# Where the first low weight part of the next stage stands at the end of the second and third feed-forward net

## The chip, the cores and the metric

The kernel runs on one core of one Trainium2 chip. The metric is device time in microseconds (us), the median over runs of the same program. Engines are named as in the profile: PE is TensorE (matmuls) and PEld its weight loads, DVE is VectorE, ACT is ScalarE, POOL is GpSimd, SP is SyncE, which here only issues DMA transfers. L76 is line 76 of the kernel before.

## The reference

Two layers act on 256 tokens of 1024 features, in float32. Each layer is a feed-forward net, a mixer, a cross-attention and a second feed-forward net, each added to its input and normalised:

```python
for l in range(DEPTH):                       # DEPTH = 2
    h = layer_norm(ALPHA * h + 0.5 * swiglu(h, ffn1_gate[l], ffn1_up[l], ffn1_down[l]), ...)
    z = h @ w_in[l]                          # conv, recurrence and pooling branches on slices of z
    ...
    h = layer_norm(ALPHA * h + mix, ...)
    h = layer_norm(ALPHA * h + cross_attn(h, mem, ca_q[l], ca_k[l], ca_v[l], ca_o[l]), ...)
    h = layer_norm(ALPHA * h + 0.5 * swiglu(h, ffn2_gate[l], ffn2_up[l], ffn2_down[l]), ...)

def swiglu(x, w_gate, w_up, w_down):         # 1024 -> 2816 -> 1024
    return (jax.nn.silu(x @ w_gate) * (x @ w_up)) @ w_down
```

The four nets in order of time are called net 1 and 2 (`ffn1`, `ffn2` of layer 0) and net 3 and 4 (of layer 1). The keys of the cross-attention come from `mem` and not from `h`, so their products need nothing of the net in front of them.

## The kernel before

**High and low parts.** Every float32 operand of a matmul is used as two parts. `split` (L74) makes them: ScalarE rounds the tile to the high part (`whi`, L75) and VectorE subtracts that from the source for the low part (`wlo`, L76). A product of two such operands is three matmuls (`mm_rows`, L156): high by high, high by low, low by high. The tensor named `acc` holds most sums, `dn` those of the nets' last products.

**Weights.** `load` (L79) brings a block of weights in two or four tiles of 128 x 1024 through a ring of six raw buffers, one transfer of 512 KB each on SP's queue, and splits each tile into one of eight `whi` and one of eight `wlo` buffers. A raw buffer is free for the next transfer when its low part is made; a `whi` or `wlo` buffer is free when TensorE has done its last matmul with it.

**The end of a net.** A net's products run over 512 hidden features at a time. Its last three slabs of down weights, six tiles of high and low parts, are kept in `end` (L849 to L859). `finish` (L326) then works through the two tiles of 128 tokens: `tile_done(0)`, then `tile_done(1)`. For each tile TensorE adds the last products (`tail`, L861), and VectorE adds the old `h` to each half of the features as the sums are done (L356), forms the mean (`mv`, L366), waits for ScalarE's sum of squares (L369), forms `rs` (L370, and a power on POOL, L374), scales (L377) and shifts (L382, the list `normed`). During tile 1's last products TensorE transposes the finished tile 0 (L199, called from L354), and the split of that gives the next stage's `xT`. `finish` returns a function that transposes tile 1 later, within the next stage (`pend`).

**The next stage.** Behind net 2 comes `first` of net 3 (L503): `load` of four gate tiles and four up tiles, then for token tile 0 the eight gate products and the first four up products, the transposes of tile 1 (`pend`, L584), and the rest. Behind net 3 comes `keys(1, 0)` (L883): `load` of four key tiles, then products with `mem`, the transposes of tile 1 among them, and then the mixer's first projection, whose weights `columns` (L911) queues behind tile 1's norm.

**What sets the order.** Each engine works through its own queue in order. The order in a queue is made ahead of time by a planner, which takes the instructions that are ready by its own estimate of times, the earlier traced one first. `tc.issue_after(ins)` adds to that: what a block traces on `ins`'s engine is queued behind `ins`. The kernel before has one such rule for the place of this change. Where the net has three blocks done by seven products instead of eight (`5 in sevens`: nets 2, 3 and 4) and it isn't the last, `finish` gets `ordered=True`: the work of tile 1 on VectorE, and the four low parts of the next block that is loaded, are queued behind tile 0's norm. The list `guard` carries that instruction from `finish` to the next `load`:

```python
first = guard.pop() if guard else None                       # L84, load
...
with tc.issue_after(first) if first else nullcontext():      # L116
    split(h, w, r)
...
tile_done(0)                                                 # L389, finish
with tc.issue_after(normed[-1].ins) if ordered else nullcontext():
    if ordered:
        guard.append(normed[-1].ins)
    tile_done(1)
```

The rule holds the low parts alone: the rounding is on ScalarE, on which `issue_after` of a VectorE instruction lays nothing.

Of the kernel before, what the change touches and what calls it, by code (L numbers as in the profile page):

```python
# [18 lines left out]
DEPTH = 2  # L19
# [4 lines left out]
NK = DM // P  # L24
# [4 lines left out]
CHUNK = 512  # L29
# [31 lines left out]
def model(ctx: ExitStack, tc: tile.TileContext, t: dict, out: bass.AP):  # L61
# [7 lines left out]
        return ps.tile(list(shape), F32, tag=tag, name=tag)  # L69


    loads, normed, lows, turns, guard = [], [], [], [], []

    def split(hi, lo, src):  # L74
        rounded = nc.scalar.copy(hi, src)  # L75
        lows.append(nc.vector.tensor_tensor(lo, src, hi.bitcast(F32), op=ALU.subtract))  # L76
        return rounded

    def load(src, k0, nk, c0, ncol, fine=False, dealt=False, across=False):  # L79


        hi, lo, todo = [], [], []
        step = 2048 // ncol
        first = guard.pop() if guard else None  # L84
        for a in range(k0, k0 + nk, step):
            half = step // 2
            raw = [
                wp.tile([P, 1024], F32, tag="raw", name="raw", bufs=6).rearrange("p (k c) -> p k c", c=ncol)
                for _ in range(2)
            ]  # L90
            part = 1 if fine else half
            for b in range(0, step, part):
                to = raw[b // half][:, b % half : b % half + part, :]
                if dealt:

                    c, u = divmod(a // 2, 2)
                    at = slice(c * CHUNK + 2 * P * b, c * CHUNK + 2 * P * (b + 1))
                    rows = src[at, c0 : c0 + ncol].rearrange("(p u) c -> p u c", u=2)[:, u, :]
                    loads.append(nc.sync.dma_start(to[:, 0, :], rows))
                elif across:  # L100
                    rows = src[:, c0 : c0 + ncol].rearrange("(p k) c -> p k c", p=P)
                    loads.append(nc.sync.dma_start(to, rows[:, a + b : a + b + part, :]))
                else:
                    loads.append(nc.sync.dma_start(
                        to, src[(a + b) * P : (a + b + part) * P, c0 : c0 + ncol].rearrange("(k p) c -> p k c", p=P)
                    ))
            for s in range(2):
                h = wp.tile([P, 1024], F32R, tag="whi", name="whi", bufs=8)
                w = wp.tile([P, 1024], F32R, tag="wlo", name="wlo", bufs=8)
                h = h.rearrange("p (k c) -> p k c", c=ncol)  # L110
                w = w.rearrange("p (k c) -> p k c", c=ncol)
                r = raw[s]
                if fine:
                    todo += [(h[:, b, :], w[:, b, :], r[:, b, :]) for b in range(half)]
                else:
                    with tc.issue_after(first) if first else nullcontext():  # L116
                        split(h, w, r)
                hi.append(h)
                lo.append(w)
        return Weights(hi, lo, half, todo)  # L120
# [50 lines left out]
    h = [cst.tile([P, DM], F32, name=f"h{i}") for i in range(NT)]  # L171
# [32 lines left out]
    def transposed(src, i, dh, dl, unit=idn, keep=None):  # L204
        for j in range(2):
            transposed_half(src, i, j, dh, dl, unit, keep)
# [116 lines left out]

    squares = kTh[:, 4:8, :].rearrange("p k c -> p (k c)")

    def finish(mm, y, scale, gb, units, last=False, junk=None, ordered=False):  # L326

        g, b = gb
        def tile_done(i):

            st = sm.tile([P, 4, 6], F32, tag="st", name="st")
            pieces, size = [slice(0, 512), slice(512, DM)], 512
            if last and i == NT - 1:

                pieces, size = [slice(0, 512), slice(512, 768), slice(768, DM)], 256
                c = slice(512, DM)  # L340
                v = halves(h[i][:, c])
                with tc.issue_after(lows[-1].ins):
                    nc.vector.scalar_tensor_tensor(v, v, ALPHA / scale, sums(y[i][1]), op0=ALU.mult, op1=ALU.add)
            for c in pieces:
                n = c.start // 512
                v = halves(h[i][:, c])
                if len(pieces) == 3 and n:
                    o = acc((P, 256))
                    mm(i, n, slice(c.start - 512, c.stop - 512), o, None)
                    nc.vector.tensor_tensor(v, v, sums(o), op=ALU.add)  # L350
                else:
                    mm(
                        i, n, slice(0, 512), None,
                        None if last or not i or not n else lambda: transposed(h[0], 0, xTh, xTl, units[0]),  # L354
                    )
                    nc.vector.scalar_tensor_tensor(  # L356
                        v, v, ALPHA / scale, sums(y[i][n]), op0=ALU.mult, op1=ALU.add,
                        accum_out=None if junk is None else st[:, n, 0:1],
                    )
                for d in range(c.start, c.stop, size):  # L360
                    if junk is None:
                        nc.vector.bn_stats(st[:, d // size, :], h[i][:, d : d + size])
            mv = sm.tile([P, 2], F32, tag="mv", name="mv")
            rs = sm.tile([P, 1], F32, tag="rs", name="rs")
            if junk is not None:
                nc.vector.tensor_scalar(  # L366
                    mv[:, 0:1], st[:, 0, 0:1], st[:, 1, 0:1], -1.0 / DM, op0=ALU.add, op1=ALU.mult
                )
                nc.scalar.activation(junk, h[i], AF.Square, bias=mv[:, 0:1], accum_out=mv[:, 1:2])  # L369
                nc.vector.tensor_scalar(rs, mv[:, 1:2], 1.0 / DM, LN_EPS / scale / scale, op0=ALU.mult, op1=ALU.add)  # L370
            else:
                nc.vector.bn_aggr(mv, st[:, 0 : DM // size, :])
                nc.vector.tensor_scalar_add(rs, mv[:, 1:2], LN_EPS / scale / scale)
            nc.gpsimd.tensor_tensor(rs, rs, nhalf[:, 0:1], op=ALU.pow)  # L374
            cs = [slice(0, 512), slice(512, DM)]
            for c in cs:
                nc.vector.scalar_tensor_tensor(  # L377
                    h[i][:, c], h[i][:, c], mv[:, 0:1], g[:, c],
                    op0=ALU.subtract if junk is None else ALU.add, op1=ALU.mult,
                )  # L380
            for c in pieces:
                normed.append(nc.vector.scalar_tensor_tensor(  # L382
                    h[i][:, c], h[i][:, c], rs, b[:, c], op0=ALU.mult, op1=ALU.add
                ))
                if last:
                    e = nc.scalar if c.start == 512 else nc.sync
                    e.dma_start(out[0, tok(i), c], h[i][:, c])

        tile_done(0)  # L389
        with tc.issue_after(normed[-1].ins) if ordered else nullcontext():  # L390
            if ordered:
                guard.append(normed[-1].ins)
            tile_done(1)
        return lambda keep=None: transposed(h[1], 1, xTh, xTl, units[1], keep)

    def project_back(slabs, late, gb, scale, unit, between=lambda: None):
# [30 lines left out]
        return finish(tail, y, scale, gb, (unit, unit), junk=squares if unit is pdn else None)  # L427


    def ffn(l, name, n, pend=None, last=False, early=None):  # L430
        gate, up, down = (t[f"{name}_{x}"][l] for x in ("gate", "up", "down"))
        with tc.tile_pool(name="ffn", bufs=2, reuse_waits="tile") as fp:
            acts = []
# [69 lines left out]
            def first():  # L503

                s = activations()
                wg = load(gate, 0, NK, 0, CHUNK, fine=pend is None)
                wu = load(up, 0, NK, 0, CHUNK) if pend is not None else None

                if pend is None:
# [366 lines left out]
                        first = alone is not None and u == 0 and k == 0  # L876
                        rows_of(a, i, k, m, first, u == 2 and k == 1, cols, alone)

            return finish(tail, ys, 0.5, gb, (idn, jdn) if name == "ffn1" else (pdn, pdn), last, None if last else squares, 5 in sevens and not last)

    def keys(l, c, between={}):  # L883
        w = load(t["ca_k"][l], 0, NK, c * CHUNK, CHUNK, across=True)
        for p in range(2):
            o = sm.tile([P, 2, SEQ], F32, tag="sums", name="sums", bufs=1)
            for j in range(2):
                between.get(4 * p + 2 * j, lambda: None)()
                add(o[:, j, :], mm_cols(w, slice((2 * p + j) * P, (2 * p + j + 1) * P), mT))
            d = slice(4 * c + 2 * p, 4 * c + 2 * p + 2)  # L890
            split(kTh[:, d, :], kTl[:, d, :], o)
# [469 lines left out]
    def beginnings(op):  # L1361
        return small_parameters(op)

    pend = None
    for l in range(DEPTH):
        pend = ffn(l, "ffn1", 0, pend, early=None if l else beginnings)
        keys(l, 0, {6: pend})
        pend = mixer(l, lambda: keys(l, 1))
        pend = attention(l, pend)
        pend = ffn(l, "ffn2", 3, pend, last=l == DEPTH - 1)  # L1370


# [25 lines left out]
```

## Time and profile before

| what | before |
|---|---|
| median of 3 runs | 1066.89 us (1066.61 to 1069.38) |
| the profiled execution's own time | 1069.4 us |
| its span, first to last instruction | 1067.7 us |
| mean granted TensorE clock | 0.996 |
| TensorE busy | 1054.8 us, 99% of the span |
| VectorE busy | 933.8 us, 87% |
| ScalarE busy | 661.6 us, 62% |
| DMA | 251.06 MB, mean 235 GB/s |

Rows of a timeline are: start in us from the span's start, us, engine, line, operation, written tensor <- read tensors, shapes, and the count of instructions merged in the row. Two instructions of a row overlap a little in the pipeline, so two casts take 2.0 us and not twice 1.04. A bracket tells how long the engine was idle ahead of the row and whose work ended that. A row of waits is: who waited <- for whom, total us, times, longest. A row of windows is one stretch: busy time of each engine with its number of instructions, then the granted TensorE clock as a share of full speed, the busy share of the DMA engines, and GB/s.

### The profile page before, as it was taken

The page shows a single profiled execution, that of the slowest core. Times are in us where ns is not written, and L with a number is a line of the kernel's source. Part 1 is how long each engine was busy: PE and PEld are TensorE (multiplying, and loading weights), DVE is VectorE, ACT ScalarE, POOL GpSimd, SP SyncE. Part 2 cuts the span into 40 slices and gives each one's busy share as a digit, 9 for nine tenths or more (in the row PEclk, how much of TensorE's full clock was granted, in tenths as well). Part 3 has the DMA queues.
Part 4 walks back from the last instruction along what each step waited for, and adds up shares of the span by engine and source line. Part 5 has one row for each costly group of instructions (what it writes and reads, how often), then busy time and mean ns, then how long its engine had stood idle before and what let it go on. Part 6 is the DMA issues. An engine that isn't in the chain of part 4 may idle for free.

```text
span 1067.7 us, 16492 instructions
## 1 busy us (share of the span) xinstructions
PE 1054.8 (99%) x6014; PEld 937.0 (88%) x6014; DVE 933.8 (87%) x1246; ACT 661.6 (62%) x909; POOL 94.6 (9%) x128
## 2 busy tenths in 40 slices
PE   9999999999999999999999999999999999999996
PEld 7888888989899888889878888888898998888896
DVE  6999898989988789888898987889899787899887
ACT  7675775676557466656665756666764665675661
POOL 8001001000000001010001001010000000000001
PEclk9999999999999999999999999999999999999999
DMA  9999984754675589988689978867636665799961
GB/s 365 291 307 288 260 270 150 262 169 151 215 275 183 163 267 251 343 202 219 227 294 252 335 218 214 269 209 242 198 111 224 243 229 176 242 290 302 239 193 69
DMA packets 142305, 251.06 MB, mean 235 GB/s; under 512 B 11248, under 2 KB 51984, under 8 KB 142224
## 3 DMA queue, kind: packets, MB, share of 16 engines
q1 hardware_dynamic: 130656, 228.89, 64.7%
q0 software_dynamic: 10992, 19.94, 10.9%
q10 hardware_dynamic: 576, 1.18, 0.3%
q8 instruction: 47, 0.77, 0.3%
q14 instruction: 34, 0.28, 0.1%
HBM read 234.50 MB, written 1.05 MB: 221 GB/s over the span
## 4 chain that ended last, share of the span: by engine, by line
PE 91%; DVE 5%; DMA 2%; issue 1%; ACT 1%; DVEq 0%; POOL 0%; ACTq 0%; SPq 0%
PE acc L132 60%; PE dn L132 28%; DVE wlo L76 2%; PE acc L199 1%; ACT whi L75 1%; PE dn L1083 0%; DMA raw<-in_w_out_dram 0%; DMA dealt<-both 0%; DVE h L382 0%; DMA raw<-in_w_in_dram 0%; PE dn L1157 0%; DMA raw<-in_ffn_down_dram 0%; DVE raw L656 0%; DMA h<-in_x_dram 0%; DVE xT L76 0%
## 5 line engine op out<-in xcount | busy, mean ns | idle before, releaser
L75 ACT CAST whi<-raw 128x1024 fp32r<-128x1024 f32 (+1 forms) x453 | 457.2, 1043 | 207.1 <-PE dn L132 58.6
L76 DVE TENSOR_TENSOR wlo<-raw,whi 128x1024 fp32r<-128x1024 f32 (+1 forms) x453 | 535.4, 1209 | 53.7 <-ACT whi L75 43.3
L132 PE MATMUL acc<-whi,xT 128*128 128x512 f32 (+1 forms) x1064 | 314.4, 373 | 0.0
L132 PEld LDWEIGHTS acc<-whi,xT 128*128 128x128 f32 x1064 | 199.5, 190 | 26.8
L132 PE MATMUL acc<-wlo,xT 128*128 128x512 f32 (+1 forms) x532 | 198.5, 373 | 1.9 <-DVE wlo L76 1.9
L132 PE MATMUL dn<-whi,ah 128*128 128x512 f32 x346 | 131.5, 380 | 0.0
L132 PE MATMUL dn<-wlo,ah 128*128 128x512 f32 x346 | 131.2, 379 | 0.1
L132 PE MATMUL dn<-whi,al 128*128 128x512 f32 x346 | 131.1, 379 | 0.0
L132 PE MATMUL acc<-xT,whi 128*128 128x512 f32 x480 | 117.7, 382 | 0.1
L132 PEld LDWEIGHTS acc<-wlo,xT 128*128 128x128 f32 x532 | 100.8, 189 | 15.6 <-DVE wlo L76 2.3
L132 PEld LDWEIGHTS acc<-xT,whi 128*128 128x128 f32 x480 | 86.7, 190 | 10.1 <-ACT whi L75 0.4
L132 PE MATMUL dn<-whi,xT 128*128 128x512 f32 x288 | 87.7, 380 | 0.0
L132 PEld LDWEIGHTS dn<-wlo,ah 128*128 128x128 f32 x346 | 65.4, 189 | 9.4 <-DVE wlo L76 0.5
L132 PEld LDWEIGHTS dn<-whi,al 128*128 128x128 f32 x346 | 65.4, 189 | 9.3
L132 PEld LDWEIGHTS dn<-whi,ah 128*128 128x128 f32 x346 | 65.4, 189 | 8.9
L132 PEld LDWEIGHTS acc<-xT,wlo 128*128 128x128 f32 x480 | 63.0, 191 | 3.8 <-DVE wlo L76 0.6
L132 PE MATMUL acc<-xT,wlo 128*128 128x256 f32 x480 | 63.5, 275 | 0.4 <-DVE wlo L76 0.4
L132 PE MATMUL acc<-wlo,kTh 128*128 128x512 f32 (+1 forms) x176 | 61.7, 351 | 0.0
L132 PE MATMUL acc<-whi,kTl 128*128 128x512 f32 (+1 forms) x176 | 61.7, 351 | 0.0
L132 PE MATMUL acc<-whi,kTh 128*128 128x512 f32 (+1 forms) x176 | 61.7, 351 | 0.0
L132 PEld LDWEIGHTS dn<-whi,xT 128*128 128x128 f32 x288 | 54.4, 189 | 7.4
L132 PE MATMUL dn<-wlo,xT 128*128 128x512 f32 x144 | 54.7, 380 | 0.1
(246 smaller groups left out, 1298.1 us busy)
## 6 DMA issues: line engine op xcount, KB each, us to landing
raw<-in_ffn_up_dram SPq DMA_DIRECT2D x88, 512.0 KB, 5.6
raw<-in_ffn_down_dram SPq DMA_DIRECT2D x88, 512.0 KB, 5.8
raw<-in_ffn_gate_dram SPq DMA_DIRECT2D x84, 512.0 KB, 5.5
raw<-in_w_in_dram SPq DMA_DIRECT2D x48, 512.0 KB, 4.6
dealt<-sg SPq DMA_DIRECT2D x80, 128.0 KB, 5.1
raw<-in_ffn_up_dram POOLq DMA_DIRECT2D x19, 512.0 KB, 6.1
raw<-in_ffn_gate_dram POOLq DMA_DIRECT2D x16, 512.0 KB, 9.9
raw<-in_ca_k_dram SPq DMA_DIRECT2D x16, 512.0 KB, 5.1
```

Source lines behind the costliest of these rows:

```text
L75: rounded = nc.scalar.copy(hi, src)
L76: lows.append(nc.vector.tensor_tensor(lo, src, hi.bitcast(F32), op=ALU.subtract))
L132: turns.append(nc.tensor.matmul(o, w, x, start=start, stop=stop, skip_group_check=more))
L199: turns.append(nc.tensor.transpose(pt[:, k, :], src[:, (4 * j + k) * P : (4 * j + k + 1) * P], unit))
```

## The change

`guard` goes. A net is now told what follows it: `ffn` gets `following`, a function that loads the next stage's first block, and calls it ahead of `finish`. The load has `hold=True`, so it issues its four transfers and keeps the four splits in `todo`. `finish` gets the block as `ahead`. It splits the first tile, queues all of tile 0's VectorE work behind that low part, and queues tile 1's work and the other three splits behind tile 0's norm. The next stage takes the block as `started`. This holds for net 2 (first gate block of net 3) and net 3 (first key block of layer 1); nets 1 and 4 have no `following`.

```diff
-    loads, normed, lows, turns, guard = [], [], [], [], []
+    loads, normed, lows, turns = [], [], [], []
...
-    def load(src, k0, nk, c0, ncol, fine=False, dealt=False, across=False):
+    def load(src, k0, nk, c0, ncol, fine=False, dealt=False, across=False, hold=False):
...
-        first = guard.pop() if guard else None
...
+                elif hold:
+                    todo.append((h, w, r))
                 else:
-                    with tc.issue_after(first) if first else nullcontext():
-                        split(h, w, r)
+                    split(h, w, r)
...
-    def finish(mm, y, scale, gb, units, last=False, junk=None, ordered=False):
+    def finish(mm, y, scale, gb, units, last=False, junk=None, ahead=None):
...
-        tile_done(0)
-        with tc.issue_after(normed[-1].ins) if ordered else nullcontext():
-            if ordered:
-                guard.append(normed[-1].ins)
+        if ahead is None:
+            tile_done(0)
             tile_done(1)
+        else:
+            split(*ahead.todo[0])
+            with tc.issue_after(lows[-1].ins):
+                tile_done(0)
+            with tc.issue_after(normed[-1].ins):
+                tile_done(1)
+                for x in ahead.todo[1:]:
+                    split(*x)
...
-    def ffn(l, name, n, pend=None, last=False, early=None):
+    def ffn(l, name, n, pend=None, last=False, early=None, started=None, following=None):
...
-                wg = load(gate, 0, NK, 0, CHUNK, fine=pend is None)
+                wg = started or load(gate, 0, NK, 0, CHUNK, fine=pend is None)
...
-            return finish(tail, ys, 0.5, gb, (idn, jdn) if name == "ffn1" else (pdn, pdn), last, None if last else squares, 5 in sevens and not last)
+            ahead = following() if following else None
+            return ahead, finish(tail, ys, 0.5, gb, (idn, jdn) if name == "ffn1" else (pdn, pdn), last, None if last else squares, ahead)
...
-    def keys(l, c, between={}):
-        w = load(t["ca_k"][l], 0, NK, c * CHUNK, CHUNK, across=True)
+    def key_weights(l, c, hold=False):
+        return load(t["ca_k"][l], 0, NK, c * CHUNK, CHUNK, across=True, hold=hold)
+
+    def keys(l, c, between={}, started=None):
+        w = started or key_weights(l, c)
...
-    pend = None
+    pend = started = None
     for l in range(DEPTH):
-        pend = ffn(l, "ffn1", 0, pend, early=None if l else beginnings)
-        keys(l, 0, {6: pend})
+        started, pend = ffn(
+            l, "ffn1", 0, pend, early=None if l else beginnings, started=started,
+            following=(lambda: key_weights(l, 0, True)) if l else None,
+        )
+        keys(l, 0, {6: pend}, started)
         pend = mixer(l, lambda: keys(l, 1))
         pend = attention(l, pend)
-        pend = ffn(l, "ffn2", 3, pend, last=l == DEPTH - 1)
+        end = l == DEPTH - 1
+        started, pend = ffn(
+            l, "ffn2", 3, pend, last=end,
+            following=None if end else lambda: load(t["ffn1_gate"][l + 1], 0, NK, 0, CHUNK, hold=True),
+        )
```

## The prediction

> **What bounds the kernel now.** I read the page first, then the list of TensorE's waits, then the two places where a net ends.
>
> ```profile
> span 1067.7 us, 16492 instructions
> PE 1054.8 (99%) x6014; PEld 937.0 (88%) x6014; DVE 933.8 (87%) x1246; ACT 661.6 (62%) x909; POOL 94.6 (9%) x128
> ```
>
> TensorE is busy 99% of the span. What a change of order can win is therefore what TensorE loses by waiting, and the waits say how little that is:
>
> ```profile
> PE acc L132 <- DVE wlo L76: 2.6, 3, 1.9
> PE dn L516 <- DVE kTh L511: 1.5, 1, 1.5
> PE acc L535 <- DMA h<-in_x_dram: 0.4, 1, 0.4
> ```
>
> The columns are total us, times, and the longest. The last two rows belong to the start. The first has three waits of TensorE for a low part; the longest, 1.9 us, stands where net 2 (the second net of layer 0) hands over to net 3. I call that place A. TensorE's timeline there:
>
> ```profile
> 528.21 1.04 PE L199 MATMUL acc<-pdn,h 128*128 128x128 f32 x8
> 529.00 0.46 PE L132 MATMUL dn<-whi,ah 128*128 128x512 f32 x1
> ...
> 531.67 0.38 PE L132 MATMUL acc<-whi,xT 128*128 128x512 f32 x1
> ...
> 537.93 0.59 PE L132 MATMUL acc<-whi,xT 128*128 128x512 f32 x2
> 540.39 0.69 PE L132 MATMUL acc<-wlo,xT 128*128 128x512 f32 x1 [1.87 <-DVE wlo L76]
> ...
> 542.58 1.71 PE L199 MATMUL acc<-pdn,h 128*128 128x128 f32 x8
> 544.05 0.46 PE L132 MATMUL acc<-whi,xT 128*128 128x512 f32 x1
> ```
>
> Net 3 begins at 531.67 with 24 matmuls on the gate weights g0 to g3, then 12 on the up weights u0 and u1, the transposes of token tile 1, and u2 and u3. From 531.67 to 537.93 are 29 starts, so one takes 0.216. The next was due at 537.93 + 2 x 0.216 = 538.36 and starts at 540.39: 2.03 us lost. Then the five matmuls to 542.58 and the eight transposes to 544.05 take 3.66 us, where five at 0.216 and one set of transposes (528.21 to 529.00, 0.79) would take 1.87: another 1.79. The reason stands in the granted clock, 0.53, in the second of these stretches (columns: busy time of PE, PEld, DVE, ACT, POOL, then clock, DMA share, GB/s):
>
> ```profile
> 538.50:540.40 1.90, 0.03 (x2) 0.01 (x1) 1.90 (x4) 0.20 (x1) 0.00 (x0) 1.00 1.03 384
> 540.40:544.05 3.65, 3.65 (x13) 3.10 (x14) 2.81 (x3) 0.37 (x1) 0.00 (x0) 0.53 1.03 365
> ...
> 560.00:1067.00 507.00, 498.60 (x2898) 443.91 (x2896) 441.68 (x587) 304.31 (x419) 35.27 (x37) 1.00 0.73 224
> ```
>
> Place A so costs 2.03 + 1.79 = 3.82 us. What ended the wait is VectorE's order:
>
> ```profile
> 519.68 1.22 DVE L76 TENSOR_TENSOR wlo<-raw,whi 128x1024 fp32r<-128x1024 f32 x1
> 521.93 0.69 DVE L356 SCALAR_TENSOR_TENSOR h<-h,dn 128x512 f32<-128x512 f32 x1 [1.04 <-PE dn L132]
> ...
> 523.23 0.69 DVE L356 SCALAR_TENSOR_TENSOR h<-h,dn 128x512 f32<-128x512 f32 x1 [0.60 <-PE dn L132]
> ...
> 525.48 0.15 DVE L370 TENSOR_SCALAR rs<-mv 128x1 f32<-128x1 f32 x1 [1.31 <-ACT kTh L369]
> ...
> 526.88 1.41 DVE L382 SCALAR_TENSOR_TENSOR h<-h,rs,lnb 128x512 f32<-128x512 f32 x2
> ...
> 528.81 2.35 DVE L76 TENSOR_TENSOR wlo<-raw,whi 128x1024 fp32r<-128x1024 f32 x2
> ...
> 532.88 1.22 DVE L76 TENSOR_TENSOR wlo<-raw,whi 128x1024 fp32r<-128x1024 f32 x1
> 534.02 0.21 DVE L366 TENSOR_SCALAR mv<-st 128x1 f32<-128x1 f32 x1
> 534.14 2.35 DVE L76 TENSOR_TENSOR wlo<-raw,whi 128x1024 fp32r<-128x1024 f32 x2
> ...
> 537.80 1.41 DVE L382 SCALAR_TENSOR_TENSOR h<-h,rs,lnb 128x512 f32<-128x512 f32 x2
> 539.12 3.49 DVE L76 TENSOR_TENSOR wlo<-raw,whi 128x1024 fp32r<-128x1024 f32 x3
> ```
>
> The eight low parts behind tile 0's norm stand as g0 g1 | g2 | g3 u0 | u1 u2 u3. The bars are tile 0's transposed parts, tile 1's statistics and tile 1's norm. From 525.48 to 542.5 VectorE has no gap. In front of that it is idle three times: 1.04 + 0.60 + 1.31 us. TensorE waits for u1, the first one behind tile 1's norm.
>
> **The change part by part.** (1) g0's low part goes ahead of tile 0's norm. It takes 1.14 us (three in 539.12 to 542.53). Its rounded input is ready:
>
> ```profile
> 518.62 2.23 ACT L75 CAST whi<-raw 128x1024 fp32r<-128x1024 f32 x2
> 527.80 2.00 ACT L75 CAST whi<-raw 128x1024 fp32r<-128x1024 f32 x2 [2.35 <-issue]
> 530.67 1.99 ACT L75 CAST whi<-raw 128x1024 fp32r<-128x1024 f32 x2
> ```
>
> These casts are, in the order of the low parts, g0 g1, g2 g3, u0 u1. g0 is rounded by 519.7. VectorE is free at 520.9, so g0's low part runs to 522.04 in the 1.04 us hole; tile 0's first addition (521.93) moves by 0.11, ends 0.69 later at 522.73, and the second still waits for TensorE at 523.23. Cost: nothing, covered by that hole. The cover lasts until the cast ends after 521.6: then the low part ends after 522.75 and the second addition slips beyond the 0.2 us by which tile 0's norm (528.29) leads the second half of its transposes (528.21 plus half of 0.79).
>
> (2) Behind tile 0's norm there is 1.14 us less work in a stretch without a gap. If the pattern of places stays, it becomes g1 g2 | g3 | u0 u1 | u2 u3: g2 is rounded by 528.85 and due at 529.95, u1 by 532.66 and due at 535.3. u1's low part then ends at 536.4, two us ahead of its use, and u2's at 540.26. TensorE reaches tile 1's transposes at 531.67 + 36 x 0.216 = 539.45, its norm ends at 539.21; u2's low part is used at 539.45 + 0.79 + 0.22 = 540.46 and is ready, with the 0.13 that u1's took to start TensorE now, at 540.39. The margins are 0.2 and 0.07, but both hold. Gain at A: all 3.82. If the pattern breaks, u1 stays behind tile 1's norm, 1.14 earlier: gain 1.14 of the wait. I take the first: mv at 534.02 waits 1.3 us for its square (the same step at 525.48), longer than one low part, so two fit ahead of its rs (the step that is at 525.48 for tile 0). What is late next is tile 1's norm itself.
>
> (3) Four transfers of 512 KB are moved in the program ahead of the closing products; on SP's queue nothing was between them and the net's last weights, so their order stays. What moves is what they free: the raw buffer of g0.
>
> ```profile
> 530.10 0.37 SPq L104 DMA_DIRECT2D raw<-in_ffn_up_dram  x1
> ```
>
> u2's transfer waits until 530.10 for it and could start at about 522.2, when g0's low part is done. That costs nothing as long as no transfer with an earlier use is behind it: the net's last weights and the dealt tile have landed by then, as the low parts that use them end at 520.9. It takes load from 538.5 to 544, where the DMA engines were at 1.03. ScalarE rounds g0 ahead of tile 0's square already, and POOL gets nothing new.
>
> (4) Place B, net 3 into the keys. The same hole is there, and what could be won is smaller:
>
> ```profile
> 689.57 1.99 ACT L75 CAST whi<-raw 128x1024 fp32r<-128x1024 f32 x2
> 690.63 1.22 DVE L76 TENSOR_TENSOR wlo<-raw,whi 128x1024 fp32r<-128x1024 f32 x1
> 692.64 0.69 DVE L356 SCALAR_TENSOR_TENSOR h<-h,dn 128x512 f32<-128x512 f32 x1 [0.79 <-PE dn L132]
> ...
> 693.93 0.69 DVE L356 SCALAR_TENSOR_TENSOR h<-h,dn 128x512 f32<-128x512 f32 x1 [0.60 <-PE dn L132]
> 704.73 0.20 DVE L366 TENSOR_SCALAR mv<-st 128x1 f32<-128x1 f32 x1
> 704.70 1.04 ACT L75 CAST whi<-raw 128x1024 fp32r<-128x1024 f32 x1 [1.32 <-DMA raw<-in_w_in_dram]
> 705.65 1.15 ACT L369 ACTIVATE kTh<-h,mv 128x1024 fp32r<-128x1024 f32 x1
> 704.86 0.49 PE L132 MATMUL acc<-mT,wlo 128*128 128x256 f32 x2 [0.36 <-DVE wlo L76]
> 717.10 0.49 PE L132 MATMUL acc<-xT,wlo 128*128 128x256 f32 x2 [0.40 <-DVE wlo L76]
> ```
>
> The key weights' first cast ends at 690.6, its low part fits at 691.85 to 692.99, and the first addition behind it ends at 693.68, ahead of 693.93. The wait of 0.36 goes, since the third key part comes 1.14 sooner. The wait of 0.40, for a low part of the next projection, lies behind tile 1's norm. That norm's square starts at 705.65, behind the cast at 704.70, though its mv is ready at 704.93; the cast waits for a transfer into a raw buffer that a key part frees, so with that part earlier the square can come up to 0.72 sooner. B gives between 0 (the second wait grows by what the first gave) and 0.76; I take 0.35, the nearest row's own wait.
>
> Sum: 3.82 + 0.35 = 4.17 us. Nothing takes it back later: TensorE has no other wait in its list, so what follows moves with it. Nets 1 and 4 keep their order. Against the profiled execution (span 1067.7, its time 1069.4) that is 1065.2; this execution is 2.5 above the median of the three, 1066.89, from which the forecast is **1062.7 us**.
>
> **The rivals.** R1: the half clock isn't in the other executions. They are 2.5 us shorter than the profiled one, and 1.79 of it could be just this. For it: the wait is short, and which executions fall below full clock I can't see. Against: the one trace has it. Then the change wins 2.03 + 0.35: 1064.5. The Trainium skill, "TensorE: Matmul & The Clock Gate", "Part 1: The HAM clock gate", states that the clock is halved after at least one idle window of about 3.4 us, and that this window runs free of the kernel. By that rule A would lose only its wait; the trace differs, with 0.53 granted behind 1.90 us of idleness.
>
> R2: the pattern breaks, by the planner's own timing of the square. The wait shrinks from 2.03 to 0.89. The waits of 0.36 and 0.40 at B cost no clock (1.00 from 560 to 1067), so the 1.79 may go too: 1.14 + 0.35, with or without 1.79, is 1063.6 or 1065.4.
>
> R3: the new low part does nothing (an order that puts the time saved into another hole): 1066.9.
>
> R4, slower: g0's low part is now a wait in front of tile 0's norm. It waits for its cast, and the cast for a transfer; behind it on VectorE stand both additions, mv, the norm, and for them TensorE's transposes:
>
> ```profile
> DMA to landing us min/median/max: 3.1/5.4/11.2
> ```
>
> That is the row of all raw transfers on SP. If the first transfer lands so late that the cast ends after 521.6 at A (now 519.7) or 692.3 at B (now 690.6), tile 0's norm and all of VectorE behind it are late by the excess x, and TensorE waits x - 0.2 at the transposes, from about 2 us on with 1.79 for the clock. At both places, x = 2.5 costs 2 x (2.5 - 0.2 + 1.79) = 8.2, less 4.2: 1070.9. Against it: the first four land in time here at both.
>
> **How the numbers follow.** Forecast 0.45, R1 0.20, R2 0.16, R3 0.05, R4 0.14. A difference of 0.3%, 3.2 us, is about what a measurement of this kernel can tell from no change. Faster by more: the forecast and half of R2, 0.53. Within: R1, the other half and R3, 0.33. Slower: R4, 0.14. The range goes from all of A and all waits at B with some 0.6 of spread, 1066.9 - 3.82 - 0.76 - 0.6 = 1061.7, to R3 with 0.3 of it, 1067.2; it leaves out R4 and little below.
>
> **What would show it.** In the changed kernel one low part stands between 520.9 and 522.1 on VectorE with tile 0's two additions still ended by TensorE; two low parts are between mv and rs; TensorE goes from net 3's first matmul to tile 1's transposes without a wait; no stretch there has a clock of 0.53; the transfer that issued at 530.10 issues near 522. The prediction is wrong if u1's low part still follows tile 1's norm, if the additions of tile 0 are ended by ScalarE or a transfer, or if a wait of like size comes up between 545 and 691, where there is none now.

## The result, and the profile after

| what | before | after |
|---|---|---|
| median | 1067.10 us (1066.16 to 1071.09, 11 runs) | 1064.43 us (1064.05 to 1065.77, 11 runs) |
| ratio to before, 95% interval | 1 | 0.9972 [0.9963, 0.9982] |
| the profiled execution's own time | 1069.4 us | 1064.4 us |
| its span | 1067.7 us | 1062.7 us |
| mean granted TensorE clock | 0.996 | 0.997 |

The change wins 2.67 us, 0.25% of the time, where 4.17 were forecast. The two profiled executions are 5.0 us apart. So most of the question is why a pair of profiles shows nearly twice what the medians show.

The first lines of the page of after:

```profile
span 1062.7 us, 16498 instructions
PE 1051.7 (99%) x6014; PEld 934.6 (88%) x6014; DVE 933.3 (88%) x1246; ACT 661.7 (62%) x909; POOL 95.0 (9%) x128
```

VectorE's busy time is within 0.5 us of before (933.3 against 933.8): nothing was taken away, an order was changed. TensorE's waits after, in the columns total us, times, longest:

```profile
PE dn L522 <- DVE kTh L517: 1.5, 1, 1.5
PE acc L541 <- DMA h<-in_x_dram: 0.5, 1, 0.5
PE acc L132 <- DVE wlo L76: 0.4, 1, 0.4
```

Of the three waits for a low part (2.6 in sum) one of 0.4 is left. The other two rows are those of the start, as before. TensorE's timeline of after at place A:

```profile
531.18 0.38 PE L132 MATMUL acc<-whi,xT 128*128 128x512 f32 x1
...
538.74 0.38 PE L132 MATMUL acc<-whi,xT 128*128 128x512 f32 x1
538.96 1.04 PE L199 MATMUL acc<-pdn,h 128*128 128x128 f32 x8
539.75 0.46 PE L132 MATMUL acc<-whi,xT 128*128 128x512 f32 x1
```

From net 3's first matmul to the first one behind tile 1's transposes are 539.75 - 531.18 = 8.57 us, and 36 matmuls of 0.216 with one set of transposes of 0.79 make 8.57: nothing is lost. In before the same stretch took 544.05 - 531.67 = 12.38. The windows of after, at the two stretches that the prediction showed of before (busy time of PE, PEld, DVE, ACT, POOL, then clock, DMA share, GB/s):

```profile
538.50:540.40 1.90, 1.90 (x14) 1.75 (x13) 1.90 (x3) 0.81 (x2) 0.00 (x0) 1.00 1.04 379
540.40:544.05 3.65, 3.65 (x19) 3.19 (x18) 3.65 (x7) 1.48 (x4) 0.00 (x0) 1.00 1.00 360
```

TensorE is busy all through, and the clock that stood at 0.53 in the second stretch is 1.00. VectorE's timeline of after shows what did it:

```profile
519.22 2.35 DVE L76 TENSOR_TENSOR wlo<-raw,whi 128x1024 fp32r<-128x1024 f32 x2
521.50 0.68 DVE L356 SCALAR_TENSOR_TENSOR h<-h,dn 128x512 f32<-128x512 f32 x1
...
522.74 0.69 DVE L356 SCALAR_TENSOR_TENSOR h<-h,dn 128x512 f32<-128x512 f32 x1 [0.56 <-PE dn L132]
...
528.32 2.35 DVE L76 TENSOR_TENSOR wlo<-raw,whi 128x1024 fp32r<-128x1024 f32 x2
...
532.39 1.22 DVE L76 TENSOR_TENSOR wlo<-raw,whi 128x1024 fp32r<-128x1024 f32 x1
533.53 0.21 DVE L366 TENSOR_SCALAR mv<-st 128x1 f32<-128x1 f32 x1
533.66 2.35 DVE L76 TENSOR_TENSOR wlo<-raw,whi 128x1024 fp32r<-128x1024 f32 x2
...
537.31 1.41 DVE L382 SCALAR_TENSOR_TENSOR h<-h,rs,lnb 128x512 f32<-128x512 f32 x2
538.63 2.35 DVE L76 TENSOR_TENSOR wlo<-raw,whi 128x1024 fp32r<-128x1024 f32 x2
```

The first row is now two low parts, the net's last and g0; the 1.04 us hole ahead of tile 0's first addition is filled, and the second addition (522.74) is still ended by TensorE. Behind it the places are g1 g2 | g3 | u0 u1 | u2 u3. The part that TensorE waited for, u1, stands ahead of tile 1's norm.

At place B the profile changed less. The rows of after, on VectorE, ScalarE and TensorE:

```profile
700.06 0.21 DVE L366 TENSOR_SCALAR mv<-st 128x1 f32<-128x1 f32 x1
702.37 0.15 DVE L370 TENSOR_SCALAR rs<-mv 128x1 f32<-128x1 f32 x1 [2.10 <-ACT kTh L369]
696.71 2.96 ACT L75 CAST whi<-raw 128x1024 fp32r<-128x1024 f32 x3
700.15 1.04 ACT L75 CAST whi<-raw 128x1024 fp32r<-128x1024 f32 x1 [0.48 <-DMA raw<-in_w_in_dram]
701.10 1.14 ACT L369 ACTIVATE kTh<-h,mv 128x1024 fp32r<-128x1024 f32 x1
712.56 0.49 PE L132 MATMUL acc<-xT,wlo 128*128 128x256 f32 x2 [0.35 <-DVE wlo L76]
```

The wait of 0.36 for a key part is gone, the one of 0.40 for the next projection is 0.35. The square of tile 1 (701.10) still stands behind a cast that waited for its transfer, though its mv is ready at 700.27.

### The profile page after: what moved, and what is told of

It is laid out like the page before. It is cut to its first block, busy times and chain, and to the rows that moved or that the text cites. A ratio compares the mean times of both kernels' runs of the same rounds, so it can differ in the third digit from the quotient of the medians.

```text
span 1062.7 us, 16498 instructions
## 1 busy us (share of the span) xinstructions
PE 1051.7 (99%) x6014; PEld 934.6 (88%) x6014; DVE 933.3 (88%) x1246; ACT 661.7 (62%) x909; POOL 95.0 (9%) x128
## 3 DMA queue, kind: packets, MB, share of 16 engines
HBM read 234.50 MB, written 1.05 MB: 222 GB/s over the span
## 4 chain that ended last, share of the span: by engine, by line
PE 97%; DVE 1%; DMA 1%; issue 0%; ACT 0%; ACTq 0%; DVEq 0%
PE acc L132 64%; PE dn L132 31%; PE acc L199 1%; DMA h<-in_x_dram 0%; PE dn L1093 0%; DVE wlo L76 0%; DMA raw<-in_w_in_dram 0%; PE dn L1167 0%; DVE h L382 0%; PE dn L1155 0%; PE dn L1166 0%; PE acc L1235 0%; DVE h L377 0%; PE dn L1118 0%; ACT kTh L369 0%
```

## The experiments

Two theories stood against each other. **Theory 1**: both terms at A, the wait of 2.03 and the half clock of 1.79, are in the executions of before; the change wins 3.8 there and gives some of it back elsewhere. **Theory 2**, rival R1 of the prediction: the half clock is in few executions, the profiled one among them; the median has only the wait in it, and the change wins about 2.1 at A. Beside them stood how much B gives, and whether the low part put ahead can delay tile 0's norm, as R4 has it.

In the table, stretch A runs from the start of tile 0's transposes to that of tile 1's in the profiled execution. The wait is the one for a low part inside that stretch.

| kernel | median (range, runs) | ratio to before, 95% interval | stretch A | wait |
|---|---|---|---|---|
| before_again | 1067.01 (1066.53 to 1069.46, 11) | 1.0001 [0.9992, 1.0010] | 13.38 | 1.87 |
| a_only | 1064.07 (1063.49 to 1065.76, 8) | 0.9972 [0.9962, 0.9983] | 11.24 | none |
| b_only | 1066.30 (1065.90 to 1066.58, 11) | 0.9990 [0.9981, 0.9999] | 13.37 | 1.87 |
| two_ahead | 1064.10 (1063.63 to 1065.59, 8) | 0.9974 [0.9964, 0.9984] | 11.50 | none |
| u1_behind | 1065.82 (1065.28 to 1067.23, 11) | 0.9988 [0.9979, 0.9997] | 13.02 | 1.52 |
| up_late | 1069.00 (1067.33 to 1070.40, 11) | 1.0016 [1.0008, 1.0025] | 15.98 | 2.79 |
| third_ahead | 1065.68 (1064.96 to 1066.82, 10) | 0.9984 [0.9975, 0.9994] | 11.49 | none |
| square_first | 1064.26 (1063.45 to 1065.26, 10) | 0.9971 [0.9962, 0.9980] | 11.24 | none |
| after_again | 1064.76 (1064.05 to 1065.71, 11) | 0.9978 [0.9969, 0.9987] | 11.24 | none |
| square_again | 1064.24 (1063.42 to 1065.42, 10) | 0.9972 [0.9963, 0.9981] | 11.23 | none |

In the first profile of before stretch A is 14.37, in that of after 11.24.

### Before once more

Nothing is edited; the kernel is profiled and timed again, to see whether another execution has the half clock.

> The kernel before, unchanged, to see its executions one by one. Theory 1 (the prediction's own sum): the half clock behind the wait at A belongs to the kernel, so every execution has a mean granted clock of about 0.996 (the changed kernel has 0.997 to 0.998), and place A costs 3.8 us in each. Theory 2 (rival R1): the half clock comes in a part of the executions only. Then most of the executions have a clock like the changed kernel's, 0.997 to 0.998, those with 0.996 are about 1.8 us longer, and a profile of one of the others has no stretch of 0.53 behind 538 and its A is 2.0 us longer than in the changed kernel and not 3.8.

TensorE's timeline and the window of the same stretch in this execution of before:

```profile
531.07 0.38 PE L132 MATMUL acc<-whi,xT 128*128 128x512 f32 x1
...
539.79 0.48 PE L132 MATMUL acc<-wlo,xT 128*128 128x512 f32 x1 [1.87 <-DVE wlo L76]
...
540.98 1.04 PE L199 MATMUL acc<-pdn,h 128*128 128x128 f32 x8
541.77 0.46 PE L132 MATMUL acc<-whi,xT 128*128 128x512 f32 x1
540.40:544.05 3.65, 3.65 (x23) 3.25 (x22) 3.65 (x6) 1.88 (x4) 0.00 (x0) 1.00 1.03 384
```

The wait is the same 1.87, and no half clock follows: the clock is 1.00, the transposes take 0.79, and the stretch from net 3's first matmul is 541.77 - 531.07 = 10.70 us. Against 8.57 in after, A costs 2.13; in the first profile of before it cost 12.38 - 8.57 = 3.81. The difference of these two is the half clock.

How many executions have it can be estimated from time and mean clock. A stretch of 3.65 us at 0.53 takes 0.47 x 3.65 = 1.7 us off 1067, 0.0016 of the mean. The mean has a second term: in all twelve profiles of this document the clock is also halved at the end of the span, behind TensorE's last matmul. In that of after:

```profile
1054.70:1056.70 2.00, 0.00 (x0) 0.00 (x0) 1.90 (x6) 0.00 (x0) 0.51 (x1) 1.00 0.00 0
1056.70:1062.70 6.00, 0.00 (x0) 0.00 (x0) 2.11 (x4) 0.00 (x0) 0.41 (x1) 0.50 0.25 89
```

There TensorE has nothing left to do, so this costs no time, but it lasts from 2.4 to 6.0 us by profile and takes 0.001 to 0.003 off the mean. The mean of after, 0.997, is this alone. A mean of 0.996 would need over 7 us of it, more than any profile has, so it points to a half clock elsewhere; an execution that has one can also read 0.997. Over 92 executions of before, those run beside these experiments, 8 have a mean clock of 0.996, and all of these took 1069.19 to 1069.98 us, 1069.41 in the median; 56 have 0.998, and took 1066.22 to 1068.64, 1066.91 in the median. Counted by time, 11 of the 92 took over 1069; the other three of these have 0.997. So the half clock is in some 9 to 12% of the executions. The first profiled execution, of 1069.4 us at 0.996, is of this kind. Theory 2 holds: two profiles of before at the same wait, one with the half clock and one without, show it. The share of executions, and that the others lost their clock at A, is inferred from time and mean clock; only a profile shows the place.

### One place alone

`a_only` keeps the new handover at net 2 and gives net 3 the old rule back; `b_only` the reverse. Shown is what each drops of the changed kernel; both put `guard` and `ordered` back for the other net.

```diff
# a_only
-            following=(lambda: key_weights(l, 0, True)) if l else None,
# b_only
-            following=None if end else lambda: load(t["ffn1_gate"][l + 1], 0, NK, 0, CHUNK, hold=True),
```

> Only net 2 loads the next stage's first weights itself (place A); net 3 keeps the rule of before. Theory 1: 3.8 us less than before in every comparison. Theory 2: about 2.0 less in the median, 3.8 against those executions that had the half clock. Both: no wait of TensorE between net 3's first matmul and tile 1's transposes, and the rest of the span as before, shifted.

> Only net 3 does it (place B); net 2 keeps the rule of before. Prediction's term: 0.35 us less (0 to 0.76). From the changed kernel's profile, where the stretch from the first key product to the end of the wait for the projection's weights is 14.84 us against 14.72 before: nothing, the wait of 0.36 goes and the wait of 0.40 grows or comes back elsewhere by as much, since tile 1's square still stands behind a cast that waits for a transfer. Both theories of the clock: the wait at A is as before.

With A alone the time is 1064.07, as good as the whole change. The waits of `a_only` for a low part, and then those of `b_only`:

```profile
PE acc L134 <- DVE wlo L76: 0.8, 2, 0.4
PE dn L134 <- DVE wlo L76: 0.5, 2, 0.3
```

```profile
PE acc L134 <- DVE wlo L76: 2.2, 2, 1.9
```

`a_only` keeps the two waits of B (0.37 and 0.42), `b_only` the wait of A (1.87); each change takes away waits at its own place alone. `b_only` keeps the second wait of B, 0.35, as after does. The second row of `a_only` is new: 0.32 at the end of net 3 and 0.20 at 802.78; the first of the two is taken up below. B alone gives 0.7 us with an interval that begins at 0.1; and none of its 11 executions had a clock of 0.996, so that its median lacks the 0.1 us that such executions add to before's (the median of all 92 is 1067.14, without the eleven over 1069 it is 1067.04). In the traces, the stretch from tile 0's transposes at B to those of the next stage is 116.33 and 116.19 us in the two profiles of before, and 116.55 and 116.07 in `a_only` and `up_late` (below), which have the old order at B too. With the new order it is 116.09 in after, 115.87 when after was profiled once more, and 116.07 in `b_only`. The means are 0.28 apart and the two groups just overlap: B gives some 0.3 us there, or less. The medians don't resolve it: A alone won 2.95 and B alone 0.7, together more than the 2.67 of the whole. The gain is A's.

### Two low parts ahead

```diff
             split(*ahead.todo[0])
+            split(*ahead.todo[1])
...
-                for x in ahead.todo[1:]:
+                for x in ahead.todo[2:]:
```

> The changed kernel with two low parts ahead of tile 0's norm instead of one. TensorE has no wait left at A that a second one could take away, so no gain. The second cast ends at 521.4 in the changed kernel, so the second low part would end at about 522.6 and the second addition (522.74) would start with next to no delay: at most 0.5 us longer at each place. If tile 0's norm had less slack than the prediction took (0.2 us), 1 us or more at each place would show as a wait of TensorE at tile 0's transposes.

VectorE and TensorE in `two_ahead`, at the end of net 2:

```profile
519.92 3.49 DVE L76 TENSOR_TENSOR wlo<-raw,whi 128x1024 fp32r<-128x1024 f32 x3
...
528.46 1.29 PE L199 MATMUL acc<-pdn,h 128*128 128x128 f32 x8
```

Three low parts, the net's last, g0 and g1, now run to 523.4 without a hole, and tile 0's norm is late for its transposes: these start 0.26 after they were due (the matmul ahead starts at 527.98 and takes 0.216) and take 1.05 instead of 0.79. That half a microsecond at A comes back at B, where the stretch is 115.39 instead of 116.09 and the wait of 0.35 is gone; tile 1's square starts there ahead of the cast that held it up in after. The median, 1064.10, isn't told apart from 1064.43. One low part is what fits the hole at A; a second gains nothing there.

### A wait of half the size

The changed kernel with the up weights' last three low parts queued behind tile 1's norm, which puts u1 back where it was late.

```diff
-                wu = load(up, 0, NK, 0, CHUNK) if pend is not None else None
+                held = bool(l) and name == "ffn1"
+                wu = load(up, 0, NK, 0, CHUNK, hold=held) if pend is not None else None
+                if held:
+                    split(*wu.todo[0])
+                    with tc.issue_after(normed[-1].ins):
+                        for x in wu.todo[1:]:
+                            split(*x)
```

> The changed kernel with u1 to u3 (net 3's second to fourth up part) held behind tile 1's norm, which is rival R2's pattern: a wait of TensorE of 1.0 to 1.6 us at A, between the changed kernel's none and the 2.0 of before. If what the wait costs is the wait alone in most executions (theory 2), the median is 1.0 to 1.7 us above the changed kernel's 1064.4, and few or no executions have the half clock. If any wait of that size costs the half clock as well (theory 1), it is 2.8 to 3.4 above.

VectorE and TensorE in `u1_behind`:

```profile
535.24 0.68 DVE L619 TENSOR_TENSOR quarters<-xT 128x512 f32<-128x512 f32 x1
...
538.74 3.49 DVE L76 TENSOR_TENSOR wlo<-raw,whi 128x1024 fp32r<-128x1024 f32 x3
540.01 0.48 PE L132 MATMUL acc<-wlo,xT 128*128 128x512 f32 x1 [1.52 <-DVE wlo L76]
```

The place that u1 had ahead of `rs` went to another operation (535.24), so u1 didn't come 1.14 sooner than in before, and the wait is 1.52, not the 0.89 of R2. The kernel takes 1.39 us more than after, about that wait. All 11 executions have a clock of 0.998 or 0.999: no sign of a half clock. At a share of 9%, though, 11 executions without one would come up about once in three times, so this doesn't show that 1.52 us is too short for it; none of the 11 of `b_only`, whose wait is 1.87, has 0.996 either.

### A longer wait

The kernel before, with all four up parts behind tile 1's norm.

```diff
-                wu = load(up, 0, NK, 0, CHUNK) if pend is not None else None
+                wu = None
+                if pend is not None:
+                    with tc.issue_after(normed[-1].ins) if l and name == "ffn1" else nullcontext():
+                        wu = load(up, 0, NK, 0, CHUNK)
```

> The kernel before with all four up parts of net 3 behind tile 1's norm: u0 is then what TensorE waits for, 2.6 to 3.2 us instead of 2.0. The wait alone makes it 0.6 to 1.2 us longer than before. If the half clock becomes likelier with the length of the wait, more than the 4 to 7 in 39 executions of before are some 1.8 us longer with a clock of 0.996, and the median moves by up to 3.0.

The timeline and windows of `up_late`:

```profile
539.99 0.49 PE L132 MATMUL acc<-wlo,xT 128*128 128x512 f32 x1 [2.79 <-DVE wlo L76]
540.00:542.00 2.00, 2.00 (x6) 1.62 (x7) 2.00 (x2) 0.00 (x0) 0.00 (x0) 0.58 0.90 323
542.00:544.00 2.00, 2.00 (x7) 1.62 (x6) 1.94 (x3) 0.00 (x0) 0.00 (x0) 0.56 0.99 317
```

The first row has the wait, grown by 0.92; the other two the half clock behind it. Stretch A grew by 2.60 against the profile of before without a half clock (15.98 against 13.38), the median by 1.7 (ratio 1.0016 [1.0008, 1.0025]), more than the wait alone. Six of the 11 executions have a clock of 0.996, four 0.997, one 0.999; behind the wait of 1.87 it was 8 of 92 at 0.996. So behind the longer wait the half clock was more frequent; neither of the two lengths has it always or never.

### The third low part ahead in place of the first

R4's mechanism: the low part put ahead has to wait for its own input. At net 2 alone, g2 goes ahead of tile 0's norm instead of g0.

```diff
-            split(*ahead.todo[0])
+            n = 2 if ahead.per == 2 and units[0] is pdn else 0
+            split(*ahead.todo[n])
...
-                for x in ahead.todo[1:]:
+                for x in ahead.todo[:n] + ahead.todo[n + 1 :]:
```

> The changed kernel, but at A the low part of g2 goes ahead of tile 0's norm instead of that of g0. Its rounded tile has to wait for a buffer that TensorE frees only within tile 1's last products (cast at 527.3 in the changed kernel). This is rival R4's mechanism with x of some 7 us: the two additions are ended by ScalarE, TensorE waits about 7 us at tile 0's transposes and goes on at half clock for about 3.6 us. 1064.4 + 7 + 1.8 = 1073 or more, slower than before. If a waiting low part did not hold up what is queued behind it, the time would stay near 1064 to 1067.

The size was a miss: I had taken g2's cast to be far later than it came. VectorE, ScalarE and TensorE in `third_ahead`:

```profile
522.63 1.23 DVE L76 TENSOR_TENSOR wlo<-raw,whi 128x1024 fp32r<-128x1024 f32 x1 [1.76 <-ACT whi L75]
523.78 0.68 DVE L356 SCALAR_TENSOR_TENSOR h<-h,dn 128x512 f32<-128x512 f32 x1
524.38 0.68 DVE L356 SCALAR_TENSOR_TENSOR h<-h,dn 128x512 f32<-128x512 f32 x1
521.56 1.99 ACT L75 CAST whi<-raw 128x1024 fp32r<-128x1024 f32 x2 [2.88 <-DMA raw<-in_ffn_gate_dram]
528.91 1.29 PE L199 MATMUL acc<-pdn,h 128*128 128x128 f32 x8 [0.82 <-DVE h L382]
```

The first cast of the ScalarE row begins at 521.56, when its transfer has landed, and ends at 522.6. VectorE stands idle for it (1.76), and the two additions are now held by nothing but the low part ahead of them. Tile 0's transposes were due at 527.94 here (the matmul ahead starts at 527.72 and takes 0.216) instead of 528.21, so the limit of 521.6 becomes 521.3: x is 1.3, and R4's price x - 0.2 is 1.1. The transposes start 0.97 late (TensorE idle for 0.82 of it) and then take 1.05 instead of 0.79, which R4 didn't have: 1.23 together. In time it is 1.25 us more than after (1065.68). So the mechanism is real and its price about as worked out; R4's half clock, from a wait of about 2 us on, was not reached. In the change the mechanism isn't met, since g0's low part doesn't wait there (the row at 519.22 of after has two low parts and no idle time).

### The square ahead of the cast at B

The changed kernel, with the projection's casts queued behind tile 1's square in layer 1.

```diff
-                nc.scalar.activation(junk, h[i], AF.Square, ...)
+                squared.append(nc.scalar.activation(junk, h[i], AF.Square, ...))
...
+                    if after is not None and l:
+                        queued.enter_context(tc.issue_after(squared[-1].ins))
```

> The changed kernel, with the casts of the mixer's first projection in layer 1 queued on ScalarE behind the square of tile 1's norm (place B). If what keeps B from gaining is that square behind a cast that waits for a transfer, mv to rs takes 1.3 us as for tile 0 instead of 2.3, and the wait of 0.35 us of TensorE for the projection's low part goes: 0.3 to 0.4 us less at B, at the edge of what the times can show. If it is the projection's low parts themselves, the wait stays or grows.

VectorE, ScalarE and TensorE in `square_first`:

```profile
703.02 0.15 DVE L370 TENSOR_SCALAR rs<-mv 128x1 f32<-128x1 f32 x1 [1.37 <-ACT kTh L369]
701.74 1.15 ACT L369 ACTIVATE kTh<-h,mv 128x1024 fp32r<-128x1024 f32 x1 [3.56 <-DVE mv L366]
712.37 1.33 PE L132 MATMUL acc<-xT,wlo 128*128 128x256 f32 x8
```

The square now starts when mv is ready; VectorE's idle time ahead of `rs` falls from 2.10 to 1.37, TensorE's wait of 0.35 is gone, and the stretch at B is 115.36 instead of 116.09. `two_ahead` has the square ahead of that cast too, and there the wait is gone and the stretch is as short, 115.39. This shows what held the wait at B.

The kernel was timed once more beside the changed one on one chip:

> The changed kernel, unchanged, on one chip and beside the same runs of before as the next kernel. 0.9972 of before, as the result has it, and no execution with the half clock: all of them with a clock of 0.997 to 0.999 and within 2 us.

> The changed kernel with the projection's casts queued behind tile 1's square at B, beside the changed kernel on the same chip. Its profile has the stretch from tile 0's transposes at B to the next ones 0.73 us shorter (115.36 against 116.09) and no wait left for a low part there. If that holds in the executions without a profile, the median is some 0.7 us below the changed kernel's; if the stretch varies by that much from execution to execution, the two are the same.

1064.24 against 1064.76 us, the ratios 0.9972 [0.9963, 0.9981] and 0.9978 [0.9969, 0.9987]. The 0.5 us go the right way, but the intervals overlap: it is faster than before, and not shown to be faster than the change.

## Why the prediction was off by 1.7 us

**Right: the place of g0, the pattern, the margins.** g0's low part runs in the 1.04 us hole and delays nothing (522.74 is ended by TensorE). The order behind is the forecast one, g1 g2 | g3 | u0 u1 | u2 u3, with two low parts between mv and `rs`. The two thin margins held: tile 1's norm ends at 538.7 for transposes at 538.96, and u2's first low product (540.05) runs on time.

**Right: the transfers.** SP's queue in after, the second and third and then the fourth transfer of up weights:

```profile
520.51 1.47 SPq L103 DMA_DIRECT2D raw<-in_ffn_up_dram  x2
529.61 0.37 SPq L103 DMA_DIRECT2D raw<-in_ffn_up_dram  x1
```

The first row holds two issues and ends at 521.98; one issue takes 0.37, as in the second row, so its second began at 521.6. That is the transfer that waited until 530.10 in before, and about 522 was forecast. No other wait came of it in this profile.

**Wrong: the sum's base.** The step that failed is "this execution is 2.5 above the median of the three, 1066.89, from which the forecast is **1062.7 us**". All of 3.82 was taken off a median, while 1.79 of it belongs to the profiled execution alone and to about one in ten others. A measured 3.81 in the profile that has the half clock, and 2.13 in the one that hasn't: the term for the wait was right, the half clock was the mis-sized term, some 0.1 us in a median instead of 1.79. That 1064.43 lies inside the stated range all the same is owed to the width of the range, which reaches up to R3's time. The sign of it stood in the text: the profiled execution was 2.5 us above the median, of which R1 took 1.79 to be the half clock. R1's time, 1064.5, is what came. Its chance of 0.20 was too low: of the three runs shown, two lay at 1066.6 and 1066.9, and the trace was of the third.

**On the page's rule.** The row is 0.53 granted behind a wait of 1.87. The Trainium skill, "TensorE: Matmul & The Clock Gate", "Part 1: The HAM clock gate", states that the clock is halved after at least one idle window of about 3.4 us, and that this window runs free of the kernel. A free window agrees with a half clock that comes in one execution and not in the next at the same wait. So does the end of the span, where the clock is halved between 2.1 and 5.1 us behind the last matmul, by profile. The length doesn't agree: the waits of 1.87 and 2.79 us and the 2.1 us at the end of after are below 3.4, and all three had half clocks. Here the measurement decides.

**Small: B.** I took 0.35 between bounds of 0 and 0.76; the profiles show some 0.3 or less, and the step that was to give the second half of it failed. The projection's third transfer did come sooner (issued at 688.22, against 700.81 in before), but then ScalarE takes one more cast ahead of the square. In before two of the projection's casts are done when it waits for the third; in after three are (the row at 696.71 above), and it waits for the fourth, whose transfer is issued where the third's was, 3.92 us ahead of mv:

```profile
701.37 2.00 ACT L75 CAST whi<-raw 128x1024 fp32r<-128x1024 f32 x2
700.81 0.37 SPq L104 DMA_DIRECT2D raw<-in_w_in_dram  x1
696.14 0.37 SPq L103 DMA_DIRECT2D raw<-in_w_in_dram  x1
```

The first two rows are of before, the last of after. So the square stayed behind a cast that waits, and `square_first` shows that this was the reason.

**Overlooked: the end of net 3.** The prediction let nothing take the gain back later. In four of the eight profiles with the new order at A (`a_only`, `u1_behind`, `third_ahead`, `square_again`) TensorE waits 0.30 to 0.43 us for a low part in net 3's last products, and in none of the four with the old order. In these four VectorE was idle 0.69 to 0.89 us for the transfer of `dealt` shortly ahead of it, in the other eight at most 0.52. So a late transfer goes with the wait; whether the earlier start of net 3 makes the margin that thin was not tested.

**The rivals.** R2 didn't come; forced by `u1_behind`, it costs a wait of 1.52 instead of 0.89, since something else took the place. R3 is excluded by the interval. R4 didn't come; forced by `third_ahead`, its price is about right at x = 1.3 (0.97 for 1.1, with 0.26 more in the transposes). The lead of tile 0's norm that it took as 0.2 is 0.3 by the rows it names (528.21 + 0.395 against 528.29), which would make the price 1.0.

**What the 5.0 us between the two profiles are.** Against the second profile of before, which has no half clock, after is 2.4 us shorter (1065.1 against 1062.7): tile 1's transposes at A start 2.02 sooner (538.96 against 540.98), those at B 2.49 sooner (705.99 against 708.48), the next stage's 2.38 sooner (810.34 against 812.72). Most of the gain is there at net 3's start, and it isn't given back. The other 2.6 are between the two profiles of before: 1.68 is the half clock (12.38 - 10.70), 0.61 is lost ahead of A (528.21 against 527.60), and the rest, 0.3, lies behind A.

## What to carry to other kernels

Before a stall is priced from one profile, set the profiled execution against the median of the runs: what makes that execution longer than the others can't be won from the median, and here the lower clock behind a wait of about 2 us was of that kind. One step of work that has its input fits a hole ahead of a norm; how long the hole is and when the input is there tell how much may go in, and each tenth beyond that is paid by everything behind it on the engine. When a wait falls with an earlier transfer, look at what else stands in the waiting engine's queue: at B the square needed its place in the queue, not the transfer.

## What the runs showed of the hardware

A wait of TensorE can be followed by some 3.4 us at half clock: the clock is 0.50 from 540.54 to 543.95 in the first profile of before and from 540.34 to 543.75 in that of `up_late`. Whether it comes differs between executions of one program: by the mean clock of 0.996, behind 1.87 us in 8 of 92, behind 2.79 us in 6 of 11; behind 1.52 us none of 11 had it, which is too few to tell from 8 of 92. At the end of the span, where TensorE has no work left, the clock was halved in every profile, 2.1 to 5.1 us behind the last matmul. I had taken the half clock that one trace showed to be in all executions.
